# Layer 0's token projection in three passes instead of five, with the second pass cut by pairs of blocks

## The chip, the cores and the metric

The kernel runs on one core of a Trainium2 chip. The metric is device time in microseconds (us) of one execution, the median over executions. TensorE multiplies into PSUM, VectorE (DVE) and ScalarE (ACT) do the elementwise work, GpSimd (POOL) does small pieces, and the queue of SyncE (SP) issues every load from HBM.

## The reference, cut to what matters

Two decoder layers of width 2048 over 256 tokens, all in float32. In each layer a vector c gives a shift, a scale and a gate through a 2048 x 6144 matrix (adaLN); the normalised input is modulated with the first two, projected once into 7192 columns, mixed by three groups of heads, projected back and added with the gate:

```python
shift, scale, gate = jnp.split(c_act @ w_ada[l] + b_ada[l], 3, axis=-1)
h = rms_norm(x, norm_w[l]) * (1.0 + scale[:, None, :]) + shift[:, None, :]
(gq, gk, gv, glr, gz, dq, dk, dv, da, db, dz, aq, ak, av, az) = jnp.split(h @ w_in[l], bounds, axis=-1)
...   # gated linear attention, gated DeltaNet, differential attention, each with its gate
y = jnp.concatenate([o_gla, o_gdn, o_diff], axis=-1) @ w_out[l]
x = x + gate[:, None, :] * y
```

## The kernel before, in words

**Loads.** All weights come as pieces of 128 x 1024 float32 (512 KB) into one ring of 6 buffers (tag `raw`, L30). Both the pieces of `w_in`/`w_out` (tile `raw`, issued in `weights`, L298) and those of `w_ada` (tile `rawa`, L320) use that ring, and SP issues them in one queue; a buffer is free again when DVE has read it.

**Float32 on TensorE.** A weight piece is split by ACT into a rounded part `wh` (L300) and by DVE into the rest `wl` (L301). Each product is three fast matmuls (`wh,hh`, `wl,hh`, `wh,hl`).

**adaLN.** The product with `w_ada` is done on DVE (L325, one multiply with a sum for each piece). A layer has 12 groups of 8 pieces; groups 0 to 7 each give shift and scale for two of the 16 row tiles ("k tiles") of h, groups 8 to 11 the gates. "Pieces done" counts these pieces from the start of the kernel: k tiles 2g and 2g+1 of layer 0 need 8(g+1) of them, the whole of layer 0 needs 96. `advance` (L1087) emits pieces and, as soon as a group is there, the modulation of its two k tiles (`modulate`, L383: on DVE `hn` and `hl`, on ACT `hh`).

**The input projection** runs in steps, `STEPS[l]` (L68): a step (b0, b1, k0, k1) takes blocks b0 to b1 over k tiles k0 to k1. Blocks 0 to 17 are called the feature blocks here (two mixed blocks of 268 columns, and 16 of 128 columns by 256 tokens); blocks 18 to 27 are the token blocks (512 columns each, 2 x 128 tokens): 18 and 19 give aq, 20 and 21 ak, 22 and 23 av, 24 gz, 25 dz, 26 and 27 az. Each block's step ends in PSUM and is copied out: by ACT in its first pass (L434), by a DVE add onto the earlier sum in every later one (L436). Layer 0 has seven steps: token blocks k 0-2, token blocks k 2-4, feature blocks k 0-4, token blocks k 4-8, token blocks k 8-12, feature blocks k 4-16, token blocks k 12-16.

**When w_ada's pieces come.** For step i `ADA_BY` (L1223) names the group that should be done by its end; the pieces are spread over the step by the share of columns done (L1163 and `block_done`). The step begins with `advance` to the group of its last k tile, so those pieces come first in any case. In the output projection they are spread over its 48 sums (`pace`, L1185, `out_span`, L1180).

**The mixers** are generators that are put between the matmuls by a clock kept in the program: DeltaNet (`gdn`) starts when the dk blocks have their last pass, linear attention when gq has, the rope of q and k when aq and ak have, and attention when av has. The output projection has three phases (`OUT_STEPS`, L73), each after the gate of its group of heads: k tiles 0-4 (linear attention), 4-8 (DeltaNet), 8-16 (attention).

**Order.** The instructions of each engine are put in order by the tile scheduler, from the program's order and the priorities that it names. Every engine then runs its own in that order.

Of the kernel before, what the change touches and what calls it, by code (L numbers as in the profile page):

```python
# [49 lines left out]
def _token_block(name, width):  # L50
# [14 lines left out]

STEPS = {0: ((18, 28, 0, 2), (18, 28, 2, 4), (0, 18, 0, 4), (18, 28, 4, 8), (18, 28, 8, 12), (0, 18, 4, 16), (18, 28, 12, 16)),  # L68
         1: ((18, 28, 0, 8), (0, 18, 0, 16), (18, 28, 8, 16))}


# [4 lines left out]
def in_chunks(layer, i):  # L76

    b0, b1, k0, k1 = STEPS[layer][i]
    out = []
    for b in range(b0, b1):  # L80
        for k in range(k0, k1):
            c = out[-1] if out else None
            if c is None or BLOCKS[c[-1][0]][0] != BLOCKS[b][0] or (k == k0 and BLOCKS[b][0] == "T") \
                    or _chunk_elems(c) + _width(b) > RAW:
                out.append([(b, k, k + 1)])
            elif c[-1][0] == b:
                c[-1] = (b, c[-1][1], k + 1)
            else:
                c.append((b, k, k + 1))
    return out  # L90
# [50 lines left out]
def hybrid_trunk(ctx: ExitStack, tc: tile.TileContext, x, cvec, pos, par, w_ada, w_in, w_out, w_lr, qkn, adt, cst, out):  # L141
# [13 lines left out]
    def t16(name, shape, dt=F32):  # L155
        return big.tile(shape, dt, name=name, tag="b16")
# [189 lines left out]
    ada_n = [0]  # L346
# [6 lines left out]
    def ada_mark(l, g):  # L353

        return 8 * (12 * l + g + 1)
# [63 lines left out]
    def project(l, group, hh, hl, o, after):  # L419
        b0, b1, k0, k1 = STEPS[l][group]  # L420
        first = k0 == 0
# [652 lines left out]
    for l in range(L):  # L1074
# [12 lines left out]
        def advance(n, l=l, xt=xt, rb=rb, hh=hh, hl=hl, mod=mod):  # L1087

            while True:
                while mod[0] < KT and ada_n[0] >= ada_mark(l, mod[0] // 2):  # L1090
                    with tc.high_priority(offset=AHEAD):
                        modulate(l, xt, rb, hh, hl, mod[0])
                    mod[0] += 2
                if ada_n[0] >= n:
                    break
                ada_to(ada_n[0] + 1)

        def block_done(b, done, last, l=l, o=o, g=g):
            kind, name, i, _ = BLOCKS[b]
            lo, hi = span  # L1100
            if l == 0 and b == STEPS[0][0][0] and len(seen) == 0:
                seen.add("constants")
# [56 lines left out]

        for i, (b0, b1, k0, k1) in enumerate(STEPS[l]):  # L1160
            advance(ada_mark(l, (k1 - 1) // 2))
            hi = ADA_BY[l][i]
            span = (ada_n[0], max(ada_n[0], ada_mark(*hi)))  # L1163
            if k1 == KT and g.scr is None:
                if l == 1:
                    SP.dma_start(xs, xt)
                g.scr = t16("scr", [P, 8, 512])
            project(l, i, hh, hl, o, block_done)
# [4 lines left out]
        for q in range(4):  # L1173
# [3 lines left out]
        DVE.tensor_scalar(dn, pcol("diff_n", 2 * l, 2), 0.2 + 0.6 * math.exp(-0.3 * l), None, ALU.mult)  # L1177
        run["gdf"] = spawn(gate_out(room, free_a, lambda: run["diff"]["done"], o.z, 1024, on_diff, od,
                                    lambda f: dn[:, f:f + 1], DVE, ot["diff"]), URG["gate"])
        out_span = (ada_n[0], ada_mark(*ADA_BY[0][-1]) if l == 0 else ada_n[0])  # L1180

        def add(c, d):
            DVE.scalar_tensor_tensor(xr[:, c, :], d, ada[l][:, 2, c:c + 1], xr[:, c, :], ALU.mult, ALU.add)  # L1183
# [36 lines left out]

QKL = 3

ADA_BY = {0: ((0, 1), (0, 2), (0, 3), (0, 5), (0, 7), (0, 11), (1, 0), (1, 2)), 1: ((1, 7), (1, 9), (1, 11))}  # L1223


# [7 lines left out]
def _layouts(i):  # L1233
# [14 lines left out]
    for l in range(L):  # L1248
        for g in range(len(STEPS[l])):
            for chunk in in_chunks(l, g):  # L1250
# [37 lines left out]
```

## Time and profile before

| | us |
|---|---|
| median of 3 runs (1105.84 to 1107.02) | 1106.91 |
| the profiled execution | 1103.98 |
| its span in the profile | 1102.2 |
| TensorE busy / VectorE busy / ScalarE busy | 1047.0 / 888.6 / 607.2 |

A page or a view of the trace is of one execution. The span runs from the first to the last instruction of the program. Matmuls are pipelined: the records of neighbours overlap, so that a row's duration is longer than the distance at which matmuls follow each other, and busy TensorE time has small losses in it that no idle time shows. The distance between two starts is what a matmul takes in a full stream.

### The profile page before, as it was taken

How to read it: one execution, taken by the hardware profiler on the slowest of the kernel's cores; microseconds unless marked ns; L12 is line 12 of the kernel's file. 1: busy time of each engine (PE TensorE's matmuls, PEld its weight loads, DVE VectorE, ACT ScalarE, POOL GpSimd, SP SyncE). 2: the span in 40 equal slices, each digit the busy share in tenths (PEclk: the TensorE clock that was granted, in tenths of full speed). 3: DMA queues.
4: the chain of work that ended last, by engine and by line, in shares of the span. 5: the costliest groups of instructions: out<-in, count | busy, mean ns of one | idle time of the engine just before them, and what ended most of it. 6: DMA issues, size and time to landing. Idle time of an engine off the chain costs nothing.

```text
span 1102.2 us, 19699 instructions
## 1 busy us (share of the span) xinstructions
PE 1047.0 (95%) x7398; PEld 918.9 (83%) x7398; DVE 888.6 (81%) x1365; ACT 607.2 (55%) x1251; POOL 219.8 (20%) x284
## 2 busy tenths in 40 slices
PE   4999999999899989999979999999999999999998
PEld 3768888889898777898977877899989877889998
DVE  5899999998999886888687776677756776787874
ACT  4745544447765646466545555468444556557742
POOL 4000000040130841134210000024222144102400
PEclk9999999999999999999998999999999999999999
DMA  9888999999877545755588888796535645777472
GB/s 352 311 299 308 351 336 341 329 296 339 301 270 254 182 145 188 249 162 186 167 318 327 308 315 319 238 306 228 181 116 174 218 164 172 246 244 236 136 216 90
DMA packets 76799, 273.24 MB, mean 248 GB/s; under 512 B 8816, under 2 KB 9888, under 8 KB 76576
## 3 DMA queue, kind: packets, MB, share of 16 engines
q1 hardware_dynamic: 76704, 271.99, 71.7%
q8 instruction: 58, 0.95, 0.3%
q14 instruction: 37, 0.30, 0.1%
HBM read 267.76 MB, written 4.19 MB: 247 GB/s over the span
## 4 chain that ended last, share of the span: by engine, by line
PE 55%; DVE 18%; DMA 11%; issue 9%; ACT 5%; POOL 2%; SPq 0%; DVEq 0%; ACTq 0%; POOLq 0%
PE pt L180 20%; PE py L180 12%; PE pf L180 12%; DMA rawa<-in_w_ada 8%; DVE wl L301 6%; DVE rawa L325 5%; DMA raw<-in_w_in 2%; ACT wh L300 2%; PE Z_ps L180 1%; PE o_gdn L180 1%; DVE fr L325 1%; PE s_ps L180 1%; DVE aqk L436 1%; DVE z L436 1%; PE o_diff L180 1%
## 5 line engine op out<-in xcount | busy, mean ns | idle before, releaser
L300 ACT CAST wh<-raw 128x1024 fp32r<-128x1024 f32 (+1 forms) x312 | 320.0, 1028 | 272.9 <-PE pt L180 119.4
L301 DVE TENSOR_TENSOR wl<-raw,wh 128x1024 fp32r<-128x1024 f32 (+1 forms) x312 | 384.1, 1236 | 72.2 <-ACT wh L300 68.9
L180 PE MATMUL pt<-wl,hh 128*128 128x512 f32 (+1 forms) x768 | 293.5, 383 | 5.4 <-DVE wl L301 5.4
L180 PE MATMUL pt<-wh,hl 128*128 128x512 f32 (+1 forms) x768 | 291.7, 382 | 0.0
L325 DVE SCALAR_TENSOR_TENSOR rawa<-rawa,c_row 128x1024 f32<-128x1024 f32 x184 | 229.1, 1250 | 74.6 <-DMA rawa<-in_w_ada 74.3
L180 PE MATMUL pt<-wh,hh 128*128 128x512 f32 (+1 forms) x768 | 273.1, 383 | 8.5 <-ACT hh L389 4.3
L180 PEld LDWEIGHTS pt<-wh,hh 128*128 128x128 f32 x768 | 145.3, 191 | 40.6 <-ACT hh L389 5.7
L180 PEld LDWEIGHTS pt<-wl,hh 128*128 128x128 f32 x768 | 145.9, 190 | 38.3 <-DVE wl L301 10.4
L180 PEld LDWEIGHTS pt<-wh,hl 128*128 128x128 f32 x768 | 146.0, 190 | 28.7 <-issue 0.2
L180 PE MATMUL pf<-hh,wl 128*128 128x256 f32 x512 | 143.4, 283 | 3.5 <-DVE wl L301 3.5
L180 PE MATMUL pf<-hh,wh 128*128 128x256 f32 x512 | 144.3, 282 | 1.7 <-ACT wh L300 1.6
L180 PE MATMUL pf<-hl,wh 128*128 128x256 f32 x512 | 144.1, 282 | 0.0
L180 PE MATMUL py<-ogg,wh 128*128 128x256 f32 x512 | 101.1, 291 | 1.2 <-DVE xr L1183 0.6
L180 PEld LDWEIGHTS pf<-hh,wl 128*128 128x128 f32 x512 | 95.6, 188 | 6.0 <-DVE wl L301 4.2
L180 PEld LDWEIGHTS pf<-hh,wh 128*128 128x128 f32 x512 | 96.1, 188 | 3.1 <-ACT wh L300 1.8
L180 PEld LDWEIGHTS pf<-hl,wh 128*128 128x128 f32 x512 | 96.0, 188 | 1.5 <-issue 1.0
L180 PE MATMUL py<-odf,wh 128*128 128x256 f32 x512 | 91.4, 282 | 1.4 <-ACT odf L1028 1.0
L180 PEld LDWEIGHTS py<-ogg,wh 128*128 128x128 f32 x512 | 81.4, 190 | 3.2 <-DVE xr L1183 0.8
L180 PEld LDWEIGHTS py<-odf,wh 128*128 128x128 f32 x512 | 79.0, 190 | 2.5 <-ACT odf L1028 1.5
L337 ACT ACTIVATE ada_j<-ada_p,pt 128x2 f32<-128x2 f32 x96 | 31.1, 324 | 80.5 <-DVE rawa L325 72.8
L180 PE MATMUL py<-odf,wl 128*128 128x256 f32 x256 | 71.9, 282 | 1.4 <-DVE wl L301 1.3
L180 PE MATMUL py<-ogg,wl 128*128 128x256 f32 x256 | 72.7, 285 | 0.0
(277 smaller groups left out, 1335.9 us busy)
## 6 DMA issues: line engine op xcount, KB each, us to landing
raw<-in_w_in SPq DMA_DIRECT2D x224, 512.0 KB, 4.8
rawa<-in_w_ada SPq DMA_DIRECT2D x184, 512.0 KB, 4.8
raw<-in_w_out SPq DMA_DIRECT2D x64, 512.0 KB, 4.2
raw<-in_w_in SPq DMA_DIRECT2D x20, 402.0 KB, 4.4
fr<-in_w_ada SPq DMA_DIRECT2D x8, 512.0 KB, 10.6
xt<-in_x SPq DMA_DIRECT2D x4, 512.0 KB, 5.6
xr<-in_x SPq DMA_DIRECT2D x4, 512.0 KB, 8.2
xs<-xr SPq DMA_DIRECT2D x1, 2048.0 KB, 10.2
```

The lines of the kernel that those rows point to most:

```text
L180: return PE.matmul(o, lhsT=lhsT, rhs=rhs, start=start, stop=stop, **kw)
L300: ACT.copy(wh, raw)
L301: DVE.tensor_tensor(wl, raw, wh.bitcast(F32), ALU.subtract)
L325: DVE.scalar_tensor_tensor(raw, raw, 1.0, cb, ALU.mult, ALU.mult, accum_out=sums[:, i:i + 1])
L337: ACT.activation(tiny("ada_j", 2), sums[:, 2 * f:2 * f + 2], AF.Identity, bias=bias, scale=scale, accum_out=o)
L436: DVE.tensor_tensor(d, src, d, ALU.add)
```

## The change

Layer 0's token blocks get three passes. The first is k 0-2 as before. Then come the feature blocks, k 0-4. The second pass is cut into five steps, one for each pair of token blocks, and each goes two k tiles further than the one before it: blocks 18-19 over k 2-6, 20-21 over k 2-8, 22-23 over k 2-10, 24-25 over k 2-12, 26-27 over k 2-14. Then come the feature blocks, k 4-16, and last the third pass, each pair over what it has left: k 6-16, 8-16, 10-16, 12-16, 14-16. `ADA_BY` now counts single pieces instead of groups, one number for each step and one for the output projection. Layer 1 keeps its steps and its numbers (160, 176, 192 are the groups that stood there). The layout of `w_in` follows `STEPS`; the number of its pieces is the same.

```diff
-STEPS = {0: ((18, 28, 0, 2), (18, 28, 2, 4), (0, 18, 0, 4), (18, 28, 4, 8), (18, 28, 8, 12), (0, 18, 4, 16), (18, 28, 12, 16)),
+STEPS = {0: ((18, 28, 0, 2), (0, 18, 0, 4), (18, 20, 2, 6), (20, 22, 2, 8), (22, 24, 2, 10), (24, 26, 2, 12), (26, 28, 2, 14),
+             (0, 18, 4, 16), (18, 20, 6, 16), (20, 22, 8, 16), (22, 24, 10, 16), (24, 26, 12, 16), (26, 28, 14, 16)),
          1: ((18, 28, 0, 8), (0, 18, 0, 16), (18, 28, 8, 16))}
...
-            span = (ada_n[0], max(ada_n[0], ada_mark(*hi)))
+            span = (ada_n[0], max(ada_n[0], hi))
...
-        out_span = (ada_n[0], ada_mark(*ADA_BY[0][-1]) if l == 0 else ada_n[0])
+        out_span = (ada_n[0], ADA_BY[0][-1] if l == 0 else ada_n[0])
...
-ADA_BY = {0: ((0, 1), (0, 2), (0, 3), (0, 5), (0, 7), (0, 11), (1, 0), (1, 2)), 1: ((1, 7), (1, 9), (1, 11))}
+
+ADA_BY = {0: (17, 29, 33, 40, 48, 57, 64, 72, 78, 84, 88, 92, 96, 120), 1: (160, 176, 192)}
```

In pieces, the old numbers of layer 0 are 16, 24, 32, 48, 64, 96, 104 for the seven steps and 120 for the output projection.

## Rows read from the trace of the kernel before

**Rows 1.** The page: span, then busy us, share and instructions by engine.
```profile
span 1102.2 us, 19699 instructions
PE 1047.0 (95%) x7398; PEld 918.9 (83%) x7398; DVE 888.6 (81%) x1365; ACT 607.2 (55%) x1251; POOL 219.8 (20%) x284
```

**Rows 2.** Windows by step of layer 0: stretch, length, busy us (instructions), clock, DMA.
```profile
core 0: us, PE busy (x) PEld busy (x) DVE busy (x) ACT busy (x) POOL busy (x), PEclk, DMA share, GB/s
27.10:58.30 31.20, 31.20 (x127) 24.87 (x128) 25.25 (x36) 23.74 (x43) 0.00 (x0) 1.00 0.86 313
58.30:92.00 33.70, 30.17 (x130) 22.58 (x129) 33.70 (x52) 13.28 (x22) 0.00 (x0) 1.00 0.81 275
92.00:121.00 29.00, 28.52 (x234) 27.88 (x233) 25.07 (x35) 19.80 (x42) 0.00 (x0) 1.00 0.98 366
...
348.00:438.50 90.50, 86.11 (x788) 69.98 (x786) 73.68 (x103) 52.85 (x154) 42.55 (x39) 0.98 0.53 172
...
120.00:235.00 115.00, 115.00 (x507) 93.28 (x506) 113.72 (x168) 54.64 (x86) 3.53 (x9) 1.00 0.94 332
58.30:235.00 176.70, 172.68 (x862) 142.93 (x861) 172.37 (x253) 86.72 (x148) 3.53 (x9) 1.00 0.92 326
235.00:348.00 113.00, 106.53 (x923) 100.52 (x922) 107.04 (x180) 67.91 (x137) 25.06 (x31) 0.98 0.85 296
438.50:582.00 143.50, 130.42 (x997) 122.25 (x996) 118.36 (x214) 77.94 (x181) 37.88 (x66) 0.95 0.66 225
```

**Rows 3.** Timeline of TensorE: start, duration, operation; token matmuls, then feature matmuls.
```profile
121.58 0.39 PE L180 MATMUL pt<-wl,hh 128*128 128x512 f32 x1
...
122.28 0.40 PE L180 MATMUL pt<-wl,hh 128*128 128x512 f32 x1
...
105.82 0.28 PE L180 MATMUL pf<-hh,wl 128*128 128x256 f32 x1
...
106.76 0.28 PE L180 MATMUL pf<-hl,wh 128*128 128x256 f32 x1
```

**Rows 4.** Timeline of DVE, neighbours: adaLN pieces, then wl and the adds, then modulation.
```profile
122.02 1.22 DVE L325 SCALAR_TENSOR_TENSOR rawa<-rawa,c_row 128x1024 f32<-128x1024 f32 x1
...
123.16 1.22 DVE L325 SCALAR_TENSOR_TENSOR rawa<-rawa,c_row 128x1024 f32<-128x1024 f32 x1
...
186.14 1.21 DVE L301 TENSOR_TENSOR wl<-raw,wh 128x1024 fp32r<-128x1024 f32 x1
187.27 1.27 DVE L436 TENSOR_TENSOR aqk<-pt,aqk 128x512 f32<-128x512 f32 x2
188.47 1.21 DVE L301 TENSOR_TENSOR wl<-raw,wh 128x1024 fp32r<-128x1024 f32 x1
...
27.82 0.87 DVE L390 SCALAR_TENSOR_TENSOR hl<-hn,ada,hh 128x256 fp32r<-128x256 f32 x2
```

**Rows 5.** Groups of DVE in 235 to 348 us: busy, mean ns, idle before, releaser.
```profile
L325 DVE SCALAR_TENSOR_TENSOR rawa<-rawa,c_row 128x1024 f32<-128x1024 f32 x32 | 40.3, 1266 | 0.9 <-DMA rawa<-in_w_ada 0.9
L301 DVE TENSOR_TENSOR wl<-raw,wh 128x1024 fp32r<-128x1024 f32 (+1 forms) x32 | 39.4, 1235 | 4.1 <-ACT wh L300 4.1
```

**Rows 6.** Waits in 235 to 348 us: total, times, longest.
```profile
ACT wh L300 <- DMA raw<-in_w_in: 12.9, 6, 4.2
```

**Rows 7.** The DMA view of 92 to 121 us: GB/s in 40 slices, and the packets.
```profile
GB/s 249 260 333 356 362 316 283 294 283 322 333 339 412 401 407 418 424 373 396 379 407 435 412 356 316 333 333 373 362 379 407 362 390 401 384 418 396 429 412 390
DMA packets 2902, 10.61 MB, mean 366 GB/s; under 512 B 319, under 2 KB 319, under 8 KB 2899
```

**Rows 8.** The mixers' ends, and the longest piece of the chain at the layers' border.
```profile
473.85 1.04 POOL L894 TENSOR_TENSOR on_gdn<-on_gdn,ss_gdn 128x512 f32<-128x512 f32 x1
...
522.16 0.69 DVE L1018 TENSOR_TENSOR z<-z,aqk 128x512 f32<-128x512 f32 x1
...
564.65 13.04 issue
```

**Rows 9.** DVE's adaLN group in the output projection of layer 0 (438.5 to 582 us).
```profile
L325 DVE SCALAR_TENSOR_TENSOR rawa<-rawa,c_row 128x1024 f32<-128x1024 f32 x24 | 31.4, 1315 | 8.3 <-DMA rawa<-in_w_ada 8.2
```

## The prediction, made before the changed kernel was run

> **What bounds the kernel now.** I read the page first: TensorE is busy for 1047.0 of 1102.2 us and DVE for 888.6 [rows 1]. That is an average over stages, so I cut layer 0 by its steps (the borders are the times of the last copy out of PSUM of each step) and asked for the busy time in each [rows 2], then for the distance between the starts of neighbouring instructions, which is what an instruction costs in a full stream [rows 3, 4].
>
> Three matmuls of a token block start within 0.70 us, so one costs 0.233 us; eight of a feature block start within 0.94 us, so one costs 0.1175 us [rows 3]. A token block over one k tile is 2 x 3 matmuls, 1.40 us; all feature blocks over one k tile are 48 matmuls and 12 of 268 columns (taken at 268/256 of the price), 7.1 us. Against that each stretch of [rows 2] loses:
> - 58.3 to 92 us, token blocks k 2-4: 20 x 1.40 = 28.0 of 33.7, loss 5.7. DVE is busy for the whole 33.7.
> - 92 to 121, feature blocks k 0-4: 28.5 of 29.0, loss 0.5.
> - the two token steps after it, 80 x 1.40 = 112 of some 114, loss 2; DVE is busy 113.72 of 115, so here both engines are full at once.
> - 235 to 348, feature blocks k 4-16: 85.5 of 113, and 27.5 for the mixers' small matmuls and the losses. 6.5 us are idle in plain sight; I take the small matmuls at 15.5 (the sum of their distances of starts), which leaves a loss of 12, between 6.5 and 27.5. DVE is busy 107.04.
> - 348 to 438.5 and 438.5 to 582: 56 + 90 (768 matmuls at 0.1175) of 234; the rest is mixers, the 13.04 us at the layers' border [rows 8] and losses that the rows don't part.
>
> So layer 0 is bound by TensorE wherever DVE keeps up, and DVE is level with it for the first 350 us.
>
> **The change part by part.** The matmuls, weight pieces, casts and modulations are the same in number; what changes is 40 adds, the order, and when the 184 adaLN pieces run.
>
> *The adds.* The token blocks are added onto earlier sums twice instead of four times: 2 x 20 DVE adds go. A pair takes 1.20 us between its neighbours [rows 4], so 0.60 each, 24 us of DVE. Where DVE was full but TensorE too (the two steps up to 235 us) this gives nothing by itself; what it gives is room for adaLN pieces earlier.
>
> *From 58.3 us to the feature blocks' second pass.* New: feature blocks k 0-4 and 80 block-tiles of the second pass, 28.5 + 112 = 140.5 us of TensorE. DVE: 47 pieces (17 to 64) x 1.14 = 53.6; 50 weight pieces' worth of wl x 1.13 = 56.5; 20 adds = 12; modulation of 14 k tiles, two operations of 0.4 each, 11.2; together 133, so 95% of TensorE's. The same sum for before (48 pieces, 60 weight pieces, 60 adds) gives 170 of 176.7, where the row says 172.37, so the sum holds. DMA: 97 pieces of 0.524 MB, 50.9 MB; at the 366 GB/s that the stretch from 92 to 121 reached as a mean (435 in its best slice) [rows 7] that is 139 us, which is level, not over. I take a loss of 4 us, as three levels that meet can't be without one; the ends are 0 and 15 (50.9 MB at the 326 GB/s of this whole stretch before [rows 2] are 156 us). Before, 8.2 were lost here. Gain 4, from -7 to +8.
>
> *Feature blocks k 4-16.* 8 adaLN pieces in it instead of 32 [rows 5]: 24 x 1.14 = 27 us of DVE gone from 107, and 12.6 MB of DMA from 33, so the 12.9 us that ACT waited for weight pieces [rows 6] have no cause left. The mixers' chains stay, with their handovers. Of 12 lost I take 3 to stay: gain 9, from 4 to 13.
>
> *Third pass and output projection.* 60 block-tiles come after the feature blocks instead of 40, 28 us that were before them. So DeltaNet, which starts in the feature blocks and ended at 474.9, 36 us into the output projection [rows 8], has 28 us more cover; av is complete with 12 block-tiles left instead of 16, 5.6 us later, but its queue of q and k ropes no longer runs beside DeltaNet, so attention (ended at 522.9) should end earlier against the third phase that waits for it. Against it: the pieces left out earlier come here. The third pass has 24 of them, the output projection 24 planned instead of 16; 8 x 1.14 = 9 us more for a DVE that was busy 118.36 of 143.5, and DVE waited 8.2 us for their DMA already [rows 9]. I take +5, from -6 to +12: the gates of phases two and three come earlier, a part is paid back to DVE.
>
> *Sum.* 4 + 9 + 5 = 18 off 1103.98, the profiled execution (span 1102.2 and 1.8 around it): 1086. The median of the runs is 2.9 above that execution: **1089 us**. The ends of the three terms, taken as independent, give 1080 to 1098 for this case.
>
> *A rule against the reading.* TensorE's weight loads are busy for only 93.28 of 115 us in the stretch up to 235 [rows 2], while its matmul distance is the shortest anywhere in the trace. The Trainium skill (Perfetto Trace Analysis, Identifying the Most-Contended Engine) says that matmul busy time misleads and that headroom is judged by the weight loads' share. By that the stretch would have 19% to give, some 20 us on top; that is the last rival below.
>
> **The rivals.**
> 1. *Each seam of the second pass costs what one cost before (slower).* The second pass has five steps and each begins with k tiles whose adaLN group is planned to be done only as the step before it ends (33 pieces for 32 needed, 40 for 40, 48 for 48, 57 for 56, 64 for 64 at the feature blocks). A late piece holds its sum, the modulation and then TensorE, which runs in order, with the DVE behind it in order too. The nearest row is 58.3 to 92, where 9 pieces, modulation and adds fell together and 5.7 us were lost. Five such losses are 28, in place of the 4: 1089 + 24 = 1113. It turns slower from 4.4 us a seam (22 lost). For it: DVE is 95% full in my sum. Against it: the newest k tile is the last one of each block's sum, so 2 to 10 block-tiles (2.8 to 14 us) lie ahead of it, and the same seam at 178 us cost nothing in sight. Chance 0.14.
> 2. *The stall only moves (same).* TensorE was full up to 235, so the adds give nothing; the 24 pieces taken out of the feature blocks hold DVE in the third pass and the output projection as they did before: 4 early, -4 or so late, 1105 to 1109. For it: the number of pieces and bytes is the same. Against it: the stretch from 348 has DMA at 172 and 225 GB/s, far from full. Chance 0.10.
> 3. *Half of it.* The feature blocks' 9 come, the 9 us of eight more pieces in the output projection are paid in full, and early 4 is left: 1103; with a part of the late gain 1098 to 1104. Chance 0.13.
> 4. *All losses go.* 8 early, 12 in the feature blocks, 12 late, 32 in all: 1075, or down to 1068 if the weight loads' share is right about headroom, since three matmuls in 0.70 us would then not be the floor. I know of no row that shows a shorter distance, so this end gets little. Chance 0.13 together, 0.03 of it for the last.
>
> **How the numbers follow.** Forecast 0.50, rivals 0.14, 0.10, 0.13, 0.13. Faster by over 0.2% (below 1104.7; 0.2% is what a measurement of this kernel can tell from no change): 0.50 + 0.13 + 0.13 = 0.76. Within 0.2%: 0.10. Slower: 0.14. The range goes from 1077 (inside rival 4, leaving some 0.06 below) to 1109 (leaving rival 1, most of 0.14, above).
>
> **What would show it.** In the changed trace: 60 adds of 128x512 for layer 0's and layer 1's token blocks instead of 100. Feature blocks k 4-16 in about 104 us instead of 113, with DVE busy near 80 and ACT's wait for weight pieces near nothing: the second term. The stretch from the first pass's end to there about 145 us: the first term; 155 and more with waits of TensorE on `hh` or `wl` at the starts of the steps would be rival 1. DeltaNet ending before the output projection begins, and the third phase without a wait for attention: the third term; DVE above 128 us in the output projection with waits for `rawa` would be rival 2 or 3. I am wrong in the working, whatever the total, if the gain stands in layer 1 or in the first 58 us.

## The result, and the profile after

The changed kernel takes 1119.71 us (median of 4 runs, 1113.41 to 1122.88) against 1106.38 for the kernel before beside it: a ratio of 1.0112, interval 1.0073 to 1.0152. It is slower by 1.1%; 1089 was forecast. The profiled execution took 1119.18.

The page of the changed kernel, span and engines (to read against [rows 1]):

```profile
span 1117.4 us, 19656 instructions
PE 1048.9 (94%) x7398; PEld 921.7 (82%) x7398; DVE 871.6 (78%) x1325; ACT 609.6 (55%) x1251; POOL 231.1 (21%) x284
```

DVE is busy for 17 us less, over 40 instructions fewer, and the span is 15.2 us longer. Windows of the changed kernel by step of layer 0, with the columns of [rows 2]: first pass's end to the feature blocks' second pass, feature blocks k 4-16, third pass, output projection, layer 1.

```profile
core 0: us, PE busy (x) PEld busy (x) DVE busy (x) ACT busy (x) POOL busy (x), PEclk, DMA share, GB/s
57.00:210.30 153.30, 143.76 (x724) 118.82 (x723) 137.81 (x201) 76.17 (x137) 15.80 (x24) 1.00 0.95 342
210.30:344.50 134.20, 129.28 (x1414) 121.67 (x1413) 95.47 (x150) 73.96 (x139) 31.34 (x31) 0.97 0.51 166
344.50:456.50 112.00, 106.02 (x539) 84.42 (x537) 96.98 (x134) 65.92 (x178) 42.56 (x35) 1.00 0.78 264
456.50:600.70 144.20, 121.98 (x895) 114.58 (x895) 122.14 (x221) 72.02 (x164) 33.45 (x54) 0.90 0.73 245
600.70:1117.40 516.70, 507.10 (x3666) 448.65 (x3666) 376.57 (x556) 286.40 (x569) 94.47 (x128) 1.00 0.66 223
```

The lengths alone mislead, because 20 block-tiles (28 us of TensorE) and many of the mixers' small matmuls changed stage. So I took from each trace, for each stage, the distance from each TensorE start to the next, and called **loss** what exceeds the usual distance of that matmul (0.235 us for 512 columns, 0.126 for 268, 0.118 for 256, 0.13 or 0.23 for the small ones). "Small" is the time of the mixers' matmuls without loss, "pieces" the adaLN pieces that DVE multiplied in the stage.

| us | before: loss, small, pieces | after: loss, small, pieces | loss, after less before |
|---|---|---|---|
| first pass's end to feature blocks k 4-16 | 7.0, -, - | 12.9, -, - | +5.9 |
| feature blocks k 4-16 | 14.5, 15.2, 32 | 15.2, 30.3, 11 | +0.7 |
| third pass | 9.1, 26.0, 10 | 12.4, 19.8, 23 | +3.3 |
| output projection | 29.6, 26.2, 24 | 39.3, 16.2, 33 | +9.7 |

The four add up to +19.6; small matmuls are 1.1 less, the stretch before 57 us 1.3 less, and layer 1 3.5 less (520.2 to 516.7). That is 13.7 of the 15.2; the rest is in distances that the records don't part. These sizes are of one execution of each kernel. Another choice of the small matmuls' usual distances lowers the losses of all output projections by about 2 us together, and layer 1 takes 514.9 to 522.0 us in the twelve kernels of this document that compute everything and have its code unchanged, so that a few us in one stage of one trace mean little. The largest item is the output projection, where the third term had put a gain.

In the output projection DVE's adaLN group of the changed kernel has this row, to read against [rows 9]:

```profile
L326 DVE SCALAR_TENSOR_TENSOR rawa<-rawa,c_row 128x1024 f32<-128x1024 f32 x34 | 42.7, 1265 | 9.6 <-DMA rawa<-in_w_ada 9.4
```

It covers ten pieces more than before (34 by this window, 33 by the stage's borders of the table). What they do to TensorE begins where attention does. Its first score product (`s_ps`) starts at 470.0 us, and the first transposed score (`aT_ps`), which DVE has to finish before, at 501.4; in the kernel before these were 467.7 and 478.4. Windows of that stretch, before and after:

```profile
467.70:478.40 10.70, 10.70 (x93) 10.70 (x92) 8.51 (x19) 8.05 (x24) 6.00 (x7) 1.00 0.59 183
470.00:501.40 31.40, 30.26 (x255) 29.67 (x254) 31.40 (x64) 17.25 (x35) 0.00 (x0) 1.00 0.80 263
```

After, DVE has no idle time in it, and this many adaLN pieces (before, one):

```profile
L326 DVE SCALAR_TENSOR_TENSOR rawa<-rawa,c_row 128x1024 f32<-128x1024 f32 x8 | 9.7, 1213 | 0.0
```

TensorE is still covered there, by the phases of the output projection that don't need attention (`py<-ogg`). It pays near 520 us, when they have run out. The timeline of TensorE in the changed kernel there (start, duration, operation, idle before and its releaser):

```profile
518.19 0.28 PE L181 MATMUL py<-ogg,wl 128*128 128x256 f32 x1
518.30 1.03 PE L181 MATMUL o_diff<-av,scr 128*128 128x256 f32 x4
522.57 0.45 PE L185 MATMUL aT_ps<-ct,scr 128*128 128x128 f32 x1 [3.24 <-DVE scr L966]
524.43 0.45 PE L185 MATMUL aT_ps<-ct,scr 128*128 128x128 f32 x1 [1.41 <-DVE scr L966]
```

And the timeline of DVE in the same kernel and place:

```profile
518.89 1.21 DVE L302 TENSOR_TENSOR wl<-raw,wh 128x1024 fp32r<-128x1024 f32 x1
520.02 0.48 DVE L1184 SCALAR_TENSOR_TENSOR xr<-py,ada,xr 128x256 f32<-128x256 f32 x1
520.42 1.21 DVE L326 SCALAR_TENSOR_TENSOR rawa<-rawa,c_row 128x1024 f32<-128x1024 f32 x1
521.56 0.08 DVE L326 DVE_READ_ACCUMULATOR rawa<-rawa,c_row 128x1 f32 x1
521.56 0.21 DVE L965 SCALAR_TENSOR_TENSOR cf<-sm,nlam,rsm 128x1 f32<-128x1 f32 x1
521.69 0.48 DVE L1184 SCALAR_TENSOR_TENSOR xr<-py,ada,xr 128x256 f32<-128x256 f32 x1
522.09 0.34 DVE L966 SCALAR_TENSOR_TENSOR scr<-scr,cf 128x128 f32<-128x128 f32 x1
```

The phases that don't need attention have their last matmul at 518.2, TensorE has only attention left to go on with, and attention's `scr` stands in DVE's queue behind a weight piece (`wl`) and an adaLN piece with no gap between them. The adaLN piece is 1.14 us of the wait of 3.24; the next wait, of 1.41, has a weight piece before it and no adaLN piece. Attention's products with `av` (`o_diff`) then go on until 536; before, `py<-ogg` ended at 513.8 and these products at 517.5, so that one covered all but 4 us of the other. By the matmul behind which it stands, 8.4 of the 9.7 us of loss are behind attention's products and the transposes (`s_ps`, `aT_ps`, `o_diff`, `oT_ps`). Two windows of the changed kernel around it and behind it:

```profile
517.50:531.00 13.50, 8.33 (x34) 6.15 (x33) 11.72 (x29) 7.72 (x26) 8.54 (x18) 0.67 0.69 227
531.00:546.00 15.00, 12.76 (x66) 11.39 (x67) 5.51 (x11) 4.51 (x13) 4.05 (x13) 0.73 0.12 35
```

The granted clock falls to 1.2 GHz at 522.1, towards the end of the 3.24 us without a matmul, and is there for most of the time to 546: means of 0.67 and 0.73, and 0.90 over the stage against 0.95 before.

### The profile page after: what moved, and what is told of

It is laid out like the page before. It is cut to its first block, busy times and chain, and to the rows that moved or that the text cites. A ratio compares the mean times of both kernels' runs of the same rounds, so it can differ in the third digit from the quotient of the medians.

```text
span 1117.4 us, 19656 instructions
## 1 busy us (share of the span) xinstructions
PE 1048.9 (94%) x7398; PEld 921.7 (82%) x7398; DVE 871.6 (78%) x1325; ACT 609.6 (55%) x1251; POOL 231.1 (21%) x284
## 4 chain that ended last, share of the span: by engine, by line
PE 56%; DVE 16%; DMA 14%; issue 8%; ACT 3%; POOL 2%; SPq 0%; DVEq 0%; ACTq 0%; POOLq 0%
PE pt L181 27%; DMA rawa<-in_w_ada 12%; PE pf L181 11%; PE py L181 9%; DVE wl L302 6%; DVE rawa L326 5%; PE o_gdn L181 1%; DMA raw<-in_w_in 1%; DVE xr L1184 1%; ACT wh L301 1%; PE Z_ps L181 1%; DVE on_gdn L658 1%; PE Y_ps L181 1%; PE S_ps L181 1%; PE ropeT_ps L185 1%
## 5 line engine op out<-in xcount | busy, mean ns | idle before, releaser
L181 PE MATMUL pt<-wh,hh 128*128 128x512 f32 (+1 forms) x768 | 270.1, 381 | 5.6 <-ACT hh L390 3.6
L181 PEld LDWEIGHTS pt<-wl,hh 128*128 128x128 f32 x768 | 145.0, 189 | 39.3 <-DVE wl L302 10.5
L181 PEld LDWEIGHTS pt<-wh,hh 128*128 128x128 f32 x768 | 144.2, 189 | 36.2 <-ACT hh L390 5.1
L181 PEld LDWEIGHTS pt<-wh,hl 128*128 128x128 f32 x768 | 144.8, 189 | 27.8 <-issue 0.3
```

The costliest lines, as they stand in the source:

```text
L181: return PE.matmul(o, lhsT=lhsT, rhs=rhs, start=start, stop=stop, **kw)
```

## The experiments

Each stands against the changed kernel unless its diff says otherwise; ratios are against the kernel before on the same chip. `ADA_BY` is written below by its last value of the feature blocks' second pass, of the third pass, and of the output projection: 72/96/120 in the changed kernel, 96/104/120 in the one before.

### The order or the plan

The change has two parts: the order of the steps, and a plan that does the adaLN pieces later (72 instead of 96 by the end of the feature blocks' second pass, 96 instead of 104 by the projection's end). The first runs take them apart.

**Steps of before, late plan.**

```diff
-STEPS = {0: ((18, 28, 0, 2), (0, 18, 0, 4), (18, 20, 2, 6), ...
+STEPS = {0: ((18, 28, 0, 2), (18, 28, 2, 4), (0, 18, 0, 4), (18, 28, 4, 8), (18, 28, 8, 12), (0, 18, 4, 16), (18, 28, 12, 16)),
-ADA_BY = {0: (17, 29, 33, 40, 48, 57, 64, 72, 78, 84, 88, 92, 96, 120), ...
+ADA_BY = {0: (16, 24, 32, 48, 64, 72, 96, 120), ...
```

> The steps of the kernel before (five passes), with only the later plan of adaLN pieces taken over: 72 instead of 96 by the end of the feature blocks k 4-16, 96 instead of 104 by the last token step, 120 by the end of the output projection. Theory A (the time is lost at the seams of the cut second pass and at attention's end, which the earlier DeltaNet leaves uncovered): the order of the mixers is as before, so the time stays near before, 1100 to 1109 us, and the feature blocks k 4-16 lose some us less than before's 113. Theory B (the time is lost because adaLN pieces were moved into the third pass and the output projection): slower like the changed kernel, 1113 to 1122 us.

Measured: 1117.45 us, 1.0098 (1.0062 to 1.0133). Windows of this run, feature blocks k 4-16, the pass after them, output projection:

```profile
233.30:363.70 130.40, 124.55 (x1392) 117.45 (x1392) 96.72 (x157) 70.60 (x125) 37.60 (x43) 0.99 0.56 181
363.70:448.90 85.20, 79.57 (x397) 61.89 (x395) 75.81 (x114) 47.35 (x154) 35.66 (x34) 0.98 0.77 259
448.90:595.90 147.00, 124.41 (x932) 117.11 (x932) 129.23 (x229) 81.60 (x193) 42.11 (x62) 0.91 0.74 248
```

With the old order of steps the later pieces alone make nearly the whole difference. The early stretch loses 6.8 as before, the feature blocks 15.1 with 30.6 of small matmuls, the output projection 38.6: as in the changed kernel. The plan is the cause, not the steps.

**New steps, plan of before from the feature blocks on.**

```diff
-ADA_BY = {0: (..., 57, 64, 72, 78, 84, 88, 92, 96, 120), ...
+ADA_BY = {0: (..., 57, 64, 96, 98, 100, 102, 103, 104, 120), ...
```

> The changed kernel's steps (three passes, pairs) with the adaLN pieces planned as before from the feature blocks k 4-16 on: 96 done at their end instead of 72, 104 at the end of the projection instead of 96, 120 as in both. So the steps alone are tried, without the later plan. Theory B (the late plan is the cost: in the old steps it alone took 12 us): 1100 to 1108 us, the feature blocks k 4-16 back to about 113 us, the output projection's loss back to 29. Theory A (the steps themselves cost): 1114 to 1122.

Measured: 1105.24 us, 1.0023 (0.9998 to 1.0049). Windows, early stretch and output projection:

```profile
57.40:210.70 153.30, 144.47 (x729) 119.59 (x729) 138.85 (x202) 76.66 (x137) 16.32 (x23) 1.00 0.96 344
445.10:581.10 136.00, 121.06 (x923) 113.68 (x923) 113.59 (x203) 74.15 (x166) 32.70 (x60) 0.94 0.68 236
```

The steps by themselves do nothing that can be told from no change: the early stretch loses 12.2 (5 more than before), third pass and output projection together 34.9 instead of 38.7. This is the mirror of the run above: the later plan on top of these steps is what takes the ratio from 1.0023 to 1.0112.

**Steps of before, pieces later in one place only.** Both have the steps of the first experiment. The first takes 24 pieces out of the feature blocks and leaves the output projection its 16 (72/104/120); the second leaves the feature blocks as before and gives the output projection 24 (96/96/120).

```diff
-ADA_BY = {0: (16, 24, 32, 48, 64, 72, 96, 120), ...
+ADA_BY = {0: (16, 24, 32, 48, 64, 72, 104, 120), ...
```

> The old steps, 24 pieces moved from the feature blocks k 4-16 into the last token step (72 and then 104, 120 at the end): the output projection keeps its 16. Theory B1 (pieces taken out of the feature blocks are the cost, since the order of the mixers' work then changes there): 1113 to 1118 us, nearly all of the 12. Theory B2 (the eight more pieces in the output projection are the cost): 1105 to 1109.

```diff
-ADA_BY = {0: (16, 24, 32, 48, 64, 72, 96, 120), ...
+ADA_BY = {0: (16, 24, 32, 48, 64, 96, 96, 120), ...
```

> The old steps, the feature blocks with their 32 pieces (96), none in the last token step (96), and 24 instead of 16 in the output projection (120). Theory B1: within 3 us of before, 1103 to 1109. Theory B2: 1111 to 1118.

Measured: 1116.17, 1.0116 (1.0084 to 1.0148), and 1116.71, 1.0118 (1.0084 to 1.0151). The output projection of the first, then of the second:

```profile
454.70:594.70 140.00, 122.35 (x941) 115.63 (x939) 123.18 (x220) 81.38 (x188) 41.18 (x63) 0.95 0.71 243
```

```profile
441.40:596.20 154.80, 134.01 (x1003) 124.42 (x1003) 125.40 (x226) 77.12 (x185) 41.51 (x66) 0.92 0.65 224
```

Either half costs 1.2% and both together 1.0%, so the halves don't add. Losses of feature blocks, last pass and output projection are 18.5, 13.7, 31.7 in the first and 15.6, 12.2, 37.7 in the second (before 14.5, 9.1, 29.6): with 8 pieces shifted into the output projection the loss is there, with 24 taken out of the feature blocks it is spread over all three. Neither theory is the whole of it. In the first, nine pieces fall between attention's first score product and its last product, which are 63.2 us apart (before, six and 49.8); in the second six, 49.5 us apart, but attention begins at 482.9 instead of 467.7.

**New steps, earlier plan (104/112/120).**

```diff
-ADA_BY = {0: (..., 57, 64, 72, 78, 84, 88, 92, 96, 120), ...
+ADA_BY = {0: (..., 57, 64, 104, 106, 108, 110, 111, 112, 120), ...
```

> The changed steps with still more pieces in the feature blocks k 4-16: 104 at their end, 112 at the end of the projection, 120 at the end of the output projection, which has 8 then. Theory B1 (a full feature stretch is what keeps the mixers out of it and the late stages light): as fast as the new steps with the old plan or up to 5 us faster, 1097 to 1105. Theory B2: 1095 to 1102, since the output projection is lighter by 8 pieces. Theory A: 1112 to 1120.

Measured: 1100.46 us, 0.9980 (0.9958 to 1.0001). Windows, feature blocks k 4-16 and output projection:

```profile
213.10:334.40 121.30, 111.50 (x938) 104.47 (x939) 115.43 (x190) 73.95 (x163) 20.61 (x22) 0.96 0.89 312
459.00:580.30 121.30, 112.00 (x902) 108.77 (x900) 103.54 (x188) 71.58 (x150) 37.11 (x60) 0.96 0.69 232
```

By its interval this can't be told from no change. 16 pieces in the output projection lose 18.5 there. But 39 in the feature blocks lose 21.6 where 31 or 32 lose 12 to 16 in the other kernels: that stage hides some 32 and no more.

### The early stretch

**adaLN's sums of two pieces on DVE instead of ACT.** If ACT's queue, which waits for pieces, holds the weight casts, this should free it.

```diff
-            ACT.activation(tiny("ada_j", 2), sums[:, 2 * f:2 * f + 2], AF.Identity, bias=bias, scale=scale, accum_out=o)
+            half = tiny("ada_j", 1)
+            with tc.high_priority(offset=AHEAD):
+                DVE.scalar_tensor_tensor(half, sums[:, 2 * f:2 * f + 1], scale, bias, ALU.mult, ALU.add)
+                DVE.scalar_tensor_tensor(o, sums[:, 2 * f + 1:2 * f + 2], scale, half, ALU.mult, ALU.add)
...   # the bias is no longer halved beforehand
```

> The changed kernel with the four short ACT operations that end each adaLN group (ada_j) replaced by eight short DVE operations, so that ACT's casts no longer stand behind an operation that waits for DVE's pieces (27.9 us of such waits from 57.7 to 211 us in the changed kernel, 5.3 us in the same steps before). Theory A1 (the seams lose time through ACT's queue: ada_j waits for the group, the next wh waits behind it, wl and TensorE behind that): the stretch 57.7 to 211 us falls from 153 to 147 us, the whole to 1112 to 1116. Rival A2 (the seams lose time because the pieces themselves, in DVE's queue, come late for their k tiles): the stretch stays within 2 us of 153 and the whole at 1117 to 1122.

Measured: 1120.11 us, 1.0122 (1.0082 to 1.0162). The early window, and from the waits in it the two longest of ACT:

```profile
57.70:211.00 153.30, 146.16 (x728) 120.46 (x727) 143.03 (x249) 67.80 (x90) 12.27 (x16) 0.99 0.95 342
```

```profile
ACT wh L301 <- PE pt L181: 36.8, 24, 2.7
ACT wh L301 <- DMA raw<-in_w_in: 32.5, 14, 6.0
```

The same 153.3 to a tenth. ACT, freed of its wait for DVE's pieces (27.9 us in the changed kernel), waits longer for TensorE (36.8 instead of 20.6) and for the weights' DMA (32.5 instead of 11.1): ACT's queue was not the bound.

**One second pass instead of five steps.**

```diff
-STEPS = {0: ((18, 28, 0, 2), (0, 18, 0, 4), (18, 20, 2, 6), ...
+STEPS = {0: ((18, 28, 0, 2), (0, 18, 0, 4), (18, 28, 2, 8), (0, 18, 4, 16), (18, 28, 8, 16)),
-ADA_BY = {0: (17, 29, 33, 40, 48, 57, 64, 72, 78, 84, 88, 92, 96, 120), ...
+ADA_BY = {0: (17, 32, 64, 72, 96, 120), ...
```

> Three passes without the cut by pairs: token blocks k 0-2, feature blocks k 0-4, token blocks k 2-8 in one step, feature blocks k 4-16, token blocks k 8-16; adaLN pieces planned at 17, 32, 64, 72, 96, 120. The number of adds is that of the changed kernel, the seams are one instead of five, and 20 block-tiles go back behind the feature blocks. Theory A: the feature blocks k 0-4 take some 4 us longer for three more pieces, the second pass loses under 2 us instead of 7.5, attention has 20 block-tiles of the third pass more behind the feature blocks but aq is complete at the same distance from its end; whole 1110 to 1117. Rival (the seams are not it): 1117 to 1122.

Measured: 1119.33 us, 1.0113 (1.0080 to 1.0146). Windows, feature blocks k 0-4 and second pass:

```profile
57.70:96.40 38.70, 33.43 (x241) 31.49 (x239) 31.21 (x48) 20.86 (x48) 0.00 (x0) 0.91 0.95 340
96.40:190.60 94.20, 86.31 (x361) 66.98 (x362) 90.47 (x138) 42.24 (x75) 2.32 (x7) 1.00 0.96 346
```

With four seams fewer the early stretch loses 20.8 instead of 12.9, with DMA at 0.95 throughout. The run doesn't price a seam by itself, since 20 block-tiles left the stretch and its adaLN pieces stayed. But its length goes with the bytes as in the changed kernel: 45.8 MB in 132.9 us, 344 GB/s. A cost of the seams isn't needed to explain it.

**adaLN's multiplications cut to 128 of 1024 columns.** The kernel leaves out seven eighths of that product for all pieces but the first eight; its loads stay. This is the test of DVE for the early stretch and for the output projection.

```diff
-                DVE.scalar_tensor_tensor(raw, raw, 1.0, cb, ALU.mult, ALU.mult, accum_out=sums[:, i:i + 1])
+                m = 1024 if raws is not None else 128
+                DVE.scalar_tensor_tensor(raw[:, 0:m], raw[:, 0:m], 1.0, cb[:, 0:m], ALU.mult, ALU.mult, accum_out=sums[:, i:i + 1])
```

> The changed kernel, every adaLN piece still loaded in full, but DVE multiplies and sums only 128 of its 1024 columns (all pieces but the first eight; shift, scale and gate are therefore not the reference's). It takes the pieces' time on DVE away, about 1 us each, and leaves their DMA, their buffers and their waits. Theory C1 (the second pass and the output projection lose time because DVE is short there): TensorE's loss from 58 us to the feature blocks falls from 12.9 to under 6 us, the loss in the output projection from 39 to under 27. Theory C2 (DMA, or the waits for it in DVE's order, is what is short): the first stays at 10 to 14, the second above 33.

Measured: 1084.17 us, 0.9811 (0.9778 to 0.9844). Windows, early stretch, feature blocks k 4-16, output projection:

```profile
57.90:212.20 154.30, 144.74 (x726) 119.17 (x725) 97.07 (x201) 77.17 (x137) 11.08 (x24) 1.00 0.93 340
212.20:338.50 126.30, 122.85 (x1392) 115.50 (x1390) 84.99 (x149) 74.06 (x139) 27.46 (x28) 1.00 0.52 175
449.50:567.30 117.80, 109.73 (x899) 107.29 (x899) 91.31 (x216) 73.38 (x165) 34.09 (x54) 0.98 0.84 299
```

Early, 41 us less of DVE change nothing. In the output projection 31 us less of DVE take 26.4 us off the stage, though DMA moves more there (299 GB/s against 245).

**The loads cut as well.**

```diff
-                    SP.dma_start(raw, w_ada[l, g, i])
+                    SP.dma_start(raw[:, 0:128], w_ada[l, g, i][:, 0:128])
```

> The kernel of the run with short multiplies, and now each piece's load is 128 of its 1024 columns too (the values are again not the reference's). What remains of the loss of that run and goes away here is DMA's. Theory C2: loss from 58 us to the feature blocks under 4 us here. Theory C1: within 3 us of the run with short multiplies alone. If neither the multiplies nor the loads matter, the loss stays at 10 to 14 in both, and the order of the instructions or the modulation is left.

Measured: 1065.14 us, 0.9639 (0.9610 to 0.9667). Windows, early stretch and output projection:

```profile
57.70:201.20 143.50, 142.29 (x725) 119.11 (x725) 94.31 (x192) 73.97 (x133) 10.47 (x24) 1.00 0.63 211
434.60:551.60 117.00, 110.86 (x896) 108.39 (x896) 92.06 (x213) 70.66 (x161) 32.97 (x54) 0.97 0.53 170
```

Now the early stretch falls to 143.5 and its loss to 2.3, while the output projection stays (117.0 after 117.8). The first is bound by the loads, the second by DVE's time. The loads alone, with full multiplications, were not cut: whether DVE, busy for 137.8 us, would then have held the early stretch is not shown.

### The late stages

**Attention's ropes planned earlier**, by smaller distances in the table that paces the mixers' steps (which holds for both layers).

```diff
-19: 3.75, 20: 6.25, 21: 7.5, 22: 3.75
+19: 2.0, 20: 4.0, 21: 5.0, 22: 2.0
```

> The changed kernel with the paces of the q and k ropes and of attention's start shortened (YW 19 to 22 from 3.75, 6.25, 7.5, 3.75 to 2, 4, 5, 2), so that attention is emitted about 26 us earlier in the program's clock. In the changed kernel the output projection's second phase is through at 518 us while attention goes on to 539. Theory A (attention is what the third phase now waits for): the stretch from the end of the projection to layer 1 falls from 143.5 by 8 to 12 us, the whole to 1106 to 1112. Rival (attention's end isn't the price; DVE with eight more pieces is): the stretch stays at 141 to 145 us and the whole at 1116 to 1122.

Measured: 1119.80 us, 1.0113 (1.0077 to 1.0149). Windows, output projection and layer 1:

```profile
459.60:594.00 134.40, 117.59 (x885) 111.20 (x885) 120.93 (x213) 72.76 (x159) 38.82 (x54) 0.92 0.78 260
594.00:1118.70 524.70, 511.28 (x3666) 450.65 (x3666) 376.27 (x556) 287.87 (x571) 96.67 (x128) 0.99 0.66 219
```

The output projection gets 9.8 us shorter, as an attention that ends late would have it, but what stands before it is 3.1 longer, layer 1 is 8.0 longer, and the sum is nothing. That the table makes layer 1 longer is not shown: it takes 523.4 us in the run with adaLN's sums on DVE too, which has the table of the changed kernel. Inconclusive for the whole; as a lever it doesn't serve.

**No piece left for the output projection**, with the steps of before (96/120/120) and with the new ones.

```diff
-ADA_BY = {0: (16, 24, 32, 48, 64, 72, 96, 120), ...
+ADA_BY = {0: (16, 24, 32, 48, 64, 96, 120, 120), ...
```

> The old steps; the feature blocks keep 32 pieces (96), the last token step gets 24 instead of 8 (120), the output projection none (120, where it had 16). In the runs so far TensorE's loss in the output projection goes with the pieces planned in it: 18.5 us with 8, 26.8 to 31.7 with 16, 37.7 to 39.3 with 24, about 1.25 us a piece. Theory D (that price holds down to none, and the third pass has room): output projection's loss 10 to 16, third pass 9 to 15, whole 1088 to 1098. Rival (what is taken out there is paid in the last token step): 1101 to 1110.

```diff
-ADA_BY = {0: (..., 57, 64, 72, 78, 84, 88, 92, 96, 120), ...
+ADA_BY = {0: (..., 57, 64, 96, 102, 108, 112, 116, 120, 120), ...
```

> The changed kernel's steps with the feature blocks at 96, the third pass at 102, 108, 112, 116 and 120, the output projection with none. Theory D: the output projection's loss 10 to 16 us, the third pass 8 to 14, and the second pass keeps its 12 to 13; whole 1090 to 1100. Rival: 1101 to 1110.

Measured: old steps 1101.65, 0.9969 (0.9952 to 0.9987); new steps **1090.72, 0.9873 (0.9849 to 0.9897)**, the fastest kernel that computes everything. The output projection of the first, then of the second:

```profile
435.60:577.20 141.60, 131.38 (x1043) 123.61 (x1042) 108.37 (x195) 81.35 (x185) 43.12 (x68) 0.98 0.53 176
```

```profile
325.50:445.10 119.60, 116.66 (x944) 93.52 (x943) 103.03 (x150) 63.66 (x172) 47.31 (x38) 1.00 0.70 235
445.10:568.90 123.80, 117.25 (x948) 112.89 (x947) 97.94 (x176) 70.75 (x153) 32.44 (x60) 0.97 0.59 201
```

(The second has its third pass above.) The first misses what its theory foretold (whole 1088 to 1098, output projection's loss 10 to 16), the second comes within it. With the new steps the third pass takes 23 pieces at a loss of 9.5 and the output projection, left with 11 that slip into it, loses 15.0. Attention's products end at 505 there, and not at 536, with `py<-ogg` going on until 511.7 to cover them. With the old steps the last pass is shorter, holds 21 pieces at 12.3, and the mixers have more left to do in the output projection (31.0 of small matmuls against 20.4). So the longer third pass is worth something, 10.9 us between these two, once the plan uses it.

**The two places apart.** What differs between the changed kernel and the best one is where 24 pieces stand in the feature blocks and where 24 stand at the end. Two more runs fill the square.

```diff
-ADA_BY = {0: (..., 57, 64, 72, 78, 84, 88, 92, 96, 120), ...
+ADA_BY = {0: (..., 57, 64, 72, 86, 98, 106, 114, 120, 120), ...
```

> The changed kernel with its 72 pieces by the end of the feature blocks k 4-16 kept, and the other 48 all in the third pass (86, 98, 106, 114, 120), none in the output projection. If the output projection's price stands by itself, that stage is at 120 to 128 us instead of 144. Theory F (a feature stretch with few pieces costs by itself, in the mixers that move into it): feature blocks and third pass together stay at 242 to 252 us, 8 to 18 above the 234 of the run with 96 and none; whole 1097 to 1108. Rival (it costs nothing, the sum of the two stages is what the pieces make it): together 232 to 238, whole 1088 to 1095.

```diff
-ADA_BY = {0: (..., 57, 64, 72, 78, 84, 88, 92, 96, 120), ...
+ADA_BY = {0: (..., 57, 64, 96, 96, 96, 96, 96, 96, 120), ...
```

> The changed kernel with 96 pieces by the end of the feature blocks k 4-16, none in the third pass, and its 24 in the output projection. Output projection 140 to 150 us. Theory F: feature blocks and third pass together 228 to 236 us instead of 246; whole 1106 to 1114, between the changed kernel and the run with 96 and 104. Rival: together 240 and more, whole 1114 to 1122.

Measured: 1117.24, 1.0115 (1.0089 to 1.0142), which neither theory foretold, and 1108.12, 1.0048 (1.0024 to 1.0073), as theory F has it. Third pass and output projection of the first, then of the second:

```profile
345.90:472.70 126.80, 110.95 (x531) 85.79 (x529) 117.01 (x175) 65.00 (x197) 47.45 (x34) 0.96 0.87 312
472.70:593.70 121.00, 112.77 (x899) 110.27 (x899) 99.35 (x178) 70.91 (x146) 33.60 (x54) 0.94 0.61 206
```

```profile
326.20:448.50 122.30, 122.30 (x984) 98.06 (x983) 81.25 (x115) 62.56 (x153) 39.43 (x38) 1.00 0.44 146
448.50:588.90 140.40, 118.80 (x911) 111.24 (x911) 118.06 (x214) 75.19 (x172) 35.33 (x60) 0.94 0.74 250
```

| us: feature blocks + third pass / output projection (ratio of the whole) | 24 planned for the output projection | none |
|---|---|---|
| 72 done at the feature blocks' end | 246.2 / 144.2 (1.0112) | 262.5 / 121.0 (1.0115) |
| 96 done there | 235.5 / 140.4 (1.0048) | 234.0 / 123.8 (0.9873) |

Along the upper row 24 pieces taken out of the output projection save 23 there and cost 16 before it, 15 of them in the third pass, which then holds 44 (loss 27.8); layer 1 is 4.6 longer in that trace, within the spread named above, and the whole is the same. Along the lower row they save 17 and the stages before are no longer, with 23 pieces in the third pass (its loss rises from 6.8 to 9.5 while 4 us of small matmuls leave it). The third pass is a cover like the feature blocks: for 23 pieces, and not for 44. What lies between wasn't tried.

## Why the prediction was wrong, point by point

**The sum.** Forecast were gains of 4, 9 and 5. Measured by loss they were -5.9, -0.7 and -13.0 (third pass and output projection). The first lies inside the ends that were given, the other two outside. The range of the sum was also too narrow by its own working: taken as independent, ends that lie 11, 5 and 11 below the three terms are 16 together, so its upper end is 1105, not 1098; the result is beyond either. And the 1068 of rival 4 doesn't follow from its row: 20 us on top of 1075 would be 1055.

**The early term** has the right stretch and the wrong size: 153.3 us instead of about 145. The step that failed is the choice of 4 between 0 and 15, and in it the sentence that DMA is "level, not over". The stretch moved 52.4 MB in 153.3 us, 342 GB/s as a mean at a share of 0.95; 52.4 MB in the 140.5 us of TensorE's work would have needed 373, above the 366 that I took from 29 us [rows 7]. Before, the same quotient was 57.6 MB over 168.5 us, 342. Moving 20 block-tiles out takes 28 us of TensorE from the stretch but only 5.2 MB (15 us at that rate). The nearest row was the mean of the whole stretch, 326 [rows 2], which gave the other end. DVE, which I had put at 133 of 140.5 and as the danger, was busy for 137.8 and didn't bind: 41 us less of it gave nothing, and cutting the loads as well gave a stretch of 143.5. The Trainium skill (DMA: Bandwidth & Descriptors, Specifications) has a limit of about 358 GB/s from HBM for a core. The long stretches (342 to 346) lie below it, but the 29 us at 366 and single slices of 435 above it [rows 7]; what holds the long ones at their rate, no run here shows.

**The feature blocks' term** came in its mechanism and not in time. DVE fell (95.5 of 134.2 us instead of 107 of 113; 80 was foretold), and ACT's wait of 12.9 for weight pieces [rows 6] is no more among the longest. Among the waits of the changed kernel in 210.3 to 344.5 us (in all, times, longest) stand:

```profile
DVE rawa L326 <- DMA rawa<-in_w_ada: 16.1, 9, 3.1
ACT wh L301 <- PE pf L181: 14.2, 10, 2.5
```

Two steps failed. The wait was taken for a cost of TensorE, which it wasn't: without it the loss is 15.2 as with it (14.5). And the stretch was taken to keep its contents, while the order is planned anew: DeltaNet's products moved into the room. The group of one of them in the feature blocks' second pass, before and then after:

```profile
L180 PE MATMUL Y_ps<-Um,C 64*64 64x64 f32 x32 | 1.1, 221 | 0.0
```

```profile
L181 PE MATMUL Y_ps<-Um,C 64*64 64x64 f32 x160 | 5.7, 221 | 0.0
```

Small matmuls in the stage went from 15.2 to 30.3 us and left the later stages. So of the 21 us more than before, 15 are moved work, 5.5 are the projection's own matmuls that crossed the stage's borders, and 0.7 are loss; of the 30 us more than the 104 that was foretold, 12 are the loss that was to go. What it means is that 24 pieces taken out of this stage gave nothing: 32 cost no more there than 11 (losses of 12.4 to 15.6 in the five kernels with 31 or 32 pieces, 15.1 to 18.5 in the four with 11 to 15). They are not free either: eleven cut ones left a loss of 11.2, and 7.1 with their loads cut as well.

**The late term** has the wrong sign. DeltaNet ended before the output projection, as foretold (its last product at 411.8 instead of 467.5). But attention began no earlier (470.0, before 467.7) and took 66 us instead of 50 from its first score product to its last product, with 14 pieces on DVE in that time instead of six, so the step "attention should end earlier" failed. The step that carries the loss is "8 x 1.14 = 9 us more for a DVE that was busy 118.36 of 143.5", which I set against cover and let a gain outweigh. It is paid in full: 9.7 more loss for 9 more pieces; that the two numbers are so close is luck, as the spread below shows. Loss of the output projection against the pieces in it, and the length of attention against the pieces that DVE multiplies in that time, in all kernels with whole pieces whose steps are these two and that differ in steps and plan alone:

| new steps | 96/120/120 | 72/120/120 | 104/112/120 | 96/104/120 | 96/96/120 | 72/96/120 (changed) |
|---|---|---|---|---|---|---|
| pieces | 11 | 11 | 16 | 24 | 30 | 33 |
| loss, us | 15.0 | 17.0 | 18.5 | 26.8 | 34.9 | 39.3 |
| pieces in attention | 0 | 0 | 3 | 7 | 12 | 14 |
| attention, us | 39.4 | 38.6 | 45.5 | 50.6 | 58.1 | 66.0 |

| steps of before | 96/120/120 | 96/104/120 (before) | 72/104/120 | 96/96/120 | 72/96/120 |
|---|---|---|---|---|---|
| pieces | 11 | 24 | 27 | 29 | 33 |
| loss, us | 22.3 | 29.6 | 31.7 | 37.7 | 38.6 |
| pieces in attention | 0 | 6 | 9 | 6 | 14 |
| attention, us | 48.0 | 49.8 | 63.2 | 49.5 | 68.0 |

Two more kernels have the changed kernel's steps and plan and 33 pieces: with adaLN's sums on DVE the output projection loses some 4 us less than the changed kernel, with the ropes planned earlier some 6 us less, so a single entry is good to some 4 us and the place of attention counts too. From 11 pieces to 33 that is 1.1 us each with the new steps (24.3 for 22) and 0.74 with the old (16.3 for 22), where more of the mixers' work is left to cover them; a piece takes 1.14 of DVE [rows 4]. That it is DVE's time and not the loads is shown by the cut multiplications: with 31 short pieces in the output projection, 12 of them in attention, attention takes 41.9 us. That the way goes through attention is shown by the last rows of the new steps, where attention grows with the pieces in it. What the other 19 of the changed kernel's 33 cost is not parted from it. The price includes what the clock loses behind TensorE's waits, and the runs don't part the two.

**The rivals.** Rival 1's 1113 lies nearest, by another mechanism: TensorE's waits for `wl` in the early stretch are 6.1 us in six, for `hh` there is none, and the run with fewer seams is explained by its bytes. Rival 2's and 3's mark, DVE above 128 us in the output projection, did not come (122.1, with 9.4 of waits for pieces), although rival 3's "paid in full" is what happened: the pieces came and mixers' work on DVE went, so the busy time told little. Rival 4's weight-load share: with loads and multiplications short, the early stretch has TensorE at 142.3 of 143.5 us at a loss of 2.3, and weight loads busy for only 119.1, a share of 0.83. The Trainium skill's rule (Perfetto Trace Analysis, Identifying the Most-Contended Engine) would still see room there. No run here shows matmuls of 512 columns following each other faster: their median distance is 0.233 or 0.234 us in all of them.

**Marks that held.** 60 adds instead of 100. Groups of DVE for the token blocks' adds over the whole changed kernel:

```profile
L437 DVE TENSOR_TENSOR z<-pt,z 128x512 f32<-128x512 f32 x24 | 16.0, 682 | 1.5 <-PE pt L181 1.4
L437 DVE TENSOR_TENSOR aqk<-pt,aqk 128x512 f32<-128x512 f32 x24 | 15.9, 685 | 3.5 <-PE pt L181 3.4
L437 DVE TENSOR_TENSOR av<-pt,av 128x512 f32<-128x512 f32 x12 | 8.0, 686 | 1.3 <-PE pt L181 1.2
```

Layer 1 and the first 58 us hold little of the difference (-3.5 and -1.3), and the first of these is within the spread of layer 1.

**What stays open.** With the same 24 pieces planned for the output projection, 72 instead of 96 at the feature blocks' end costs 10.7 us in feature blocks and third pass together. That size is measured. Whether it comes from DVE waiting for single pieces (16.1 us for 11 of them, 0.9 for 32 [rows 5]) or from the pieces beside the mixers in the third pass is not settled; short multiplications and short loads take 8 of the 15.2 us of loss off the feature blocks, about half each. Nor is it settled why either half of the late plan costs as much as both.

## What to carry to other kernels

A background operation that may run at any time is not free wherever an engine has idle time: count it at full price in a stage whose last chain runs through that engine (here 0.74 to 1.1 us for each piece of 1.14 us in the output projection), and at little where the chain runs elsewhere (32 pieces in the feature blocks, 23 in the third pass). So when an order of steps is changed, move the background work to the covers first: the same steps are worth nothing with the old plan, 1.1% of loss with a late one, and 1.3% of gain (1090.72 us) with none planned for the output projection, where the steps of before gain 0.3% by the same move. Call a resource that is "level" a bound, and take its rate from the mean of the longest full stretch, not from a short one.

## What the runs showed of the hardware

DMA of this core, at a share of 0.93 to 0.96 over the early stretch, moves 340 to 346 GB/s, mostly in loads of 0.5 MB, in the seven kernels with full loads whose token blocks have three passes and whose early windows were read, with DVE busy for 97 to 143 us beside it; slices of 0.7 us reach 435 [rows 7]. And in a wait of TensorE of 3.24 us, with DVE as the releaser, the granted clock fell to 1.2 GHz at 522.1 us; its means were 0.67 and 0.73 in the two windows from 517.5 to 546, which hold further waits.
